# Output projection of a two-layer encoder from seven block products instead of eight, with weight sums made by adding loads

## The chip, the core and the metric

The kernel runs on one core of a Trainium2 chip. The metric is the device time of one launch in microseconds (us), the median over several runs. The core has a matrix engine (PE), a vector engine (DVE), a scalar engine (ACT), a general engine (POOL) and a queue engine (SP) that issues loads and stores; POOL's queue can issue them too. Each engine works its own instructions in the order in which they stand, and waits on semaphores for the others. Operands lie in SBUF, 128 partitions wide; PE writes its sums into PSUM.

## The reference, cut to what matters

```python
D_MODEL = 1024; SEQ = 512; DEPTH = 2
def reference(x, w_in, pre_g, post_g, ..., w_branch, gate_b, w_out):
    for l in range(DEPTH):
        xn = rmsnorm(x, pre_g[l])
        proj = xn @ w_in[l]
        ...
        br = jnp.einsum('bsnc,ncd->bsnd', ys, w_branch[l])
        gates = jax.nn.sigmoid(g_logits.reshape(B, S, N_BRANCH, D) + gate_b[l])
        merged = jnp.sum(gates * br, axis=2)
        x = x + rmsnorm(merged @ w_out[l], post_g[l])
    return x
```

`merged @ w_out[l]` is the output projection: 512 x 1024 by 1024 x 1024, once in each layer, all in float32.

## The kernel before

Every float32 product is made of three matmuls. Each operand is split into a high part, rounded to the type that PE reads, and a low part, the rest; `mm3` multiplies high by high, high by low and low by high. For a weight tile (128 x 1024), `split_raw` does the split: ACT casts the loaded tile into `whi` (line 102), then DVE or POOL subtracts that from the loaded tile into `wlo` (line 107). With `pool=True` the subtractions go to DVE and POOL in turn, with `pool=False` to DVE alone. Four buffers each hold `whi` and `wlo`, three hold loaded tiles, and three PSUM buffers (`pm`) hold the sums of a unit while they are read.

A layer ends with two stages. The gate stage makes the merged rows `mrg`, feature by feature (8 groups of 128 features, `m`, by 512 rows); its last group is finished by DVE at line 254. The output projection follows. Before it, every `mrg[:, m]` is split into `A_h` (ACT, line 700) and `A_l` (DVE, line 701). Then for each half `hf` of the output columns (512) four weight tiles are loaded (512 KB each) and split with `pool=False`, and for each block `tb` of 128 rows a unit of 24 matmuls, 128 x 512, runs. ACT squares the unit's sum with an accumulator (line 725), DVE multiplies it by the post-norm weight (line 727). After the second half, DVE adds the two accumulators (line 135), POOL raises to the power -0.5 (line 136), and DVE writes the block's new rows with two instructions (line 735), which SP stores.

In layer 0 the next layer's first step is woven in: `norm_x(tb)` squares the new rows (ACT, line 160), scales them (DVE, line 164), has PE transpose them (line 167) and splits the result into `A_h` (ACT, line 172) and `A_l` (DVE, line 173). After it comes `mla_down`, the first projection of the next layer, with four weight tiles of 128 x 832 (`wqd`, split at lines 102 and 107) and 24 matmuls of 416 columns for each block. The last unit of layer 1 is cut into two halves of 256 columns.

The order on an engine is not the order of the source alone: a scheduler sets it when the kernel is built, by what it takes each instruction to last. It is the same on every run.

The loop of the projection:

```python
for hf in range(2):
    po = [split_w(wout[l, hf, j], 1024, False) for j in range(4)]
    for tb in range(TB):
        ...
        for k, (c0, c1) in enumerate(parts):
            ps = tm_unit(po, BW, tb, c0, c1)[:, :c1 - c0]
            if hf == 1 and l < L - 1 and tb > 0:
                norm_x(tb - 1, cl[l + 1])
            s_.activation(out=tmp_t()[:, :c1 - c0], in_=ps, func=AF.Square, ...)
            v_.tensor_tensor(out=o[:, c0:c1], in0=ps, in1=pg[hf][:, c0:c1], op=ALU.mult)
```

Of the kernel before, what the change touches and what calls it, by code (L numbers as in the profile page):

```python
# [40 lines left out]
def trunk_kernel(ctx, tc, x, wtm, wqd, wrv, wqk, wfm, wgate, wbr, wout,  # L41
# [555 lines left out]

    for l in range(L):
        c = cl[l]
        qk, zc, zb, st = {}, {}, {}, {}  # L600
# [98 lines left out]
        for m in range(KT):
            s_.activation(out=A_h[:, m, :], in_=mrg[:, m, :], func=AF.Copy, scale=0.25)  # L700
            v_.scalar_tensor_tensor(out=A_l[:, m, :], in0=mrg[:, m, :], scalar=0.25, in1=f32(A_h[:, m, :]),
                                    op0=ALU.mult, op1=ALU.subtract)
# [6 lines left out]
        sss = []  # L709
        for tb in range(TB):  # L710
            nc.sync.dma_start(out=x_rows(tb), in_=xsrc[tb * P:(tb + 1) * P, :].rearrange("p (a b) -> p a b", a=2))
        for hf in range(2):
# [1 line left out]
            for tb in range(TB):

                parts = [(0, 256), (256, 512)] if (l, hf, tb) == (L - 1, 1, TB - 1) else [(0, 512)]
                if hf == 0:
                    sss.append(small("sso", 3))
                ss = sss[tb]
                o = YT[:, tb, :] if hf == 0 else tmp_t()  # L720
                for k, (c0, c1) in enumerate(parts):
                    ps = tm_unit(po, BW, tb, c0, c1)[:, :c1 - c0]
                    if hf == 1 and l < L - 1 and tb > 0:
                        norm_x(tb - 1, cl[l + 1])
                    s_.activation(out=tmp_t()[:, :c1 - c0], in_=ps, func=AF.Square, scale=D ** -0.5,
                                  accum_out=ss[:, hf + k:hf + k + 1])
                    v_.tensor_tensor(out=o[:, c0:c1], in0=ps, in1=pg[hf][:, c0:c1], op=ALU.mult)
                if hf == 0:
                    continue
                if len(parts) == 2:  # L730
                    v_.tensor_tensor(out=ss[:, 1:2], in0=ss[:, 1:2], in1=ss[:, 2:3], op=ALU.add)
                r = rstd_rows(ss)
                xr = x_rows(tb)
                for k, src in enumerate((YT[:, tb, :], o)):
                    v_.scalar_tensor_tensor(out=xr[:, k, :], in0=src, scalar=r[:, 0:1], in1=xr[:, k, :],
                                            op0=ALU.mult, op1=ALU.add)
                    nc.sync.dma_start(out=xdst[tb * P:(tb + 1) * P, k * 512:(k + 1) * 512], in_=xr[:, k, :])
# [85 lines left out]
```

## Time and profile before

| what | value |
|---|---|
| median of 3 runs | 1084.35 us (1083.19 to 1084.37) |
| the profiled execution | 1084.56 us |
| its span, first to last instruction | 1082.8 us |
| PE busy | 1057.6 us, 98% of the span, 5096 matmuls |
| DVE busy | 645.8 us, 60% |
| ACT busy | 529.7 us, 49% |
| POOL busy | 234.2 us, 22% |
| output projection | about 499 to 546 us (layer 0), 1032 to 1077 us (layer 1) |

Busy time is the time in which an engine has an instruction running. A row of the timeline gives start, duration, engine, line, operation and `out<-in`; `xN` joins N instructions in a row; in brackets stands how long the engine sat idle before it and what released it. Matmuls overlap: one lasts longer than the distance to the next, and the distance is what it costs.

### The profile page before, as it was taken

The page shows a single profiled execution, that of the slowest core. Times are in us where ns is not written, and L with a number is a line of the kernel's source. Part 1 is how long each engine was busy: PE and PEld are TensorE (multiplying, and loading weights), DVE is VectorE, ACT ScalarE, POOL GpSimd, SP SyncE. Part 2 cuts the span into 40 slices and gives each one's busy share as a digit, 9 for nine tenths or more (in the row PEclk, how much of TensorE's full clock was granted, in tenths as well). Part 3 has the DMA queues.
Part 4 walks back from the last instruction along what each step waited for, and adds up shares of the span by engine and source line. Part 5 has one row for each costly group of instructions (what it writes and reads, how often), then busy time and mean ns, then how long its engine had stood idle before and what let it go on. Part 6 is the DMA issues. An engine that isn't in the chain of part 4 may idle for free.

```text
span 1082.8 us, 14199 instructions
## 1 busy us (share of the span) xinstructions
PE 1057.6 (98%) x5096; PEld 885.7 (82%) x5096; DVE 645.8 (60%) x1332; ACT 529.7 (49%) x1073; POOL 234.2 (22%) x249
## 2 busy tenths in 40 slices
PE   6999999999999999999999999999999999999997
PEld 5887878888888888888788787788888888888886
DVE  5774776666466654345577756675666665634443
ACT  6444576555454553224573644664544545432331
POOL 2311132221123232210033111331212323221000
PEclk9999999999999999999999999999999999999999
DMA  7221132223232223334343222213223322323342
GB/s 242 79 102 59 55 105 81 70 87 107 78 98 88 78 88 107 98 114 159 106 136 101 99 76 66 88 59 88 88 78 107 88 82 86 105 78 98 107 156 78
DMA packets 37703, 104.65 MB, mean 97 GB/s; under 512 B 5376, under 2 KB 6400, under 8 KB 37632
## 3 DMA queue, kind: packets, MB, share of 16 engines
q1 hardware_dynamic: 37632, 103.74, 30.6%
q8 instruction: 40, 0.66, 0.2%
q14 instruction: 31, 0.25, 0.1%
HBM read 99.53 MB, written 4.19 MB: 96 GB/s over the span
## 4 chain that ended last, share of the span: by engine, by line
PE 43%; ACT 3%; DVE 2%; issue 1%; DMA 1%; POOL 1%; POOLq 0%; DVEq 0%; ACTq 0%
PE pm L114 12%; PE pm L113 12%; PE pm L115 12%; PE pt L361 2%; PE po L379 1%; PE po L378 1%; DMA wraw<-in_wgate_dram 0%; ACT whi L102 0%; PE ps_s L419 0%; PE ps_s L418 0%; PE ps_s L436 0%; PE ps_s L438 0%; PE ps_s L437 0%; ACT tmp L160 0%; DMA wraw<-in_sgu_wt_dram 0%
## 5 line engine op out<-in xcount | busy, mean ns | idle before, releaser
L102 ACT CAST whi<-wraw 128x1024 fp32r<-128x1024 f32 (+3 forms) x194 | 177.4, 916 | 250.8 <-PE pm L114 149.0
L113 PE MATMUL pm<-A_h,whi 128*128 128x512 f32 x640 | 257.0, 402 | 0.0
L115 PE MATMUL pm<-A_h,wlo 128*128 128x512 f32 x640 | 249.8, 390 | 0.0
L114 PE MATMUL pm<-A_l,whi 128*128 128x512 f32 x640 | 249.5, 390 | 0.0
L107 DVE TENSOR_TENSOR wlo<-wraw,whi 128x1024 fp32r<-128x1024 f32 (+3 forms) x130 | 152.1, 1172 | 108.6 <-ACT whi L102 107.5
L107 POOL TENSOR_TENSOR wlo<-wraw,whi 128x1024 fp32r<-128x1024 f32 (+1 forms) x64 | 116.2, 1815 | 370.2 <-ACT whi L102 303.6
L113 PE MATMUL pm<-whi,A_h 128*128 128x512 f32 (+2 forms) x456 | 176.6, 388 | 2.2 <-ACT A_h L172 2.2
L114 PE MATMUL pm<-wlo,A_h 128*128 128x512 f32 (+2 forms) x456 | 175.1, 384 | 1.1 <-DVE wlo L107 1.0
L115 PE MATMUL pm<-whi,A_l 128*128 128x512 f32 (+2 forms) x456 | 175.0, 384 | 0.4
L115 PEld LDWEIGHTS pm<-A_h,wlo 128*128 128x128 f32 x640 | 120.2, 188 | 26.0
L114 PEld LDWEIGHTS pm<-A_l,whi 128*128 128x128 f32 x640 | 120.5, 188 | 22.4
L113 PEld LDWEIGHTS pm<-A_h,whi 128*128 128x128 f32 x640 | 120.3, 188 | 22.0
L113 PEld LDWEIGHTS pm<-whi,A_h 128*128 128x128 f32 x456 | 86.1, 189 | 19.0 <-ACT A_h L172 4.1
L114 PEld LDWEIGHTS pm<-wlo,A_h 128*128 128x128 f32 x456 | 86.4, 189 | 16.6 <-DVE wlo L107 2.6
L115 PEld LDWEIGHTS pm<-whi,A_l 128*128 128x128 f32 x456 | 86.1, 189 | 16.5 <-DVE A_l L173 1.9
L354 DVE TENSOR_SCALAR pp<-pp,st 128x128 f32<-128x128 f32 (+3 forms) x128 | 70.3, 549 | 3.6
L367 ACT CAST PT_h<-pt 128x128 fp32r<-128x128 f32 (+3 forms) x128 | 54.0, 423 | 29.6 <-PE pt L361 28.7
L368 DVE TENSOR_TENSOR PT_l<-pt,PT_h 128x128 fp32r<-128x128 f32 (+3 forms) x128 | 61.6, 481 | 6.7 <-ACT PT_h L367 6.3
L423 DVE CUSTOM_DVE_ANT_0 pp<-ps_s,bk 128x128 f32<-128x128 f32 (+1 forms) x64 | 31.2, 488 | 56.7 <-PE ps_s L419 56.3
L361 PE MATMUL pt<-ident,pp 128*128 128x128 f32 x320 | 55.8, 272 | 1.5 <-DVE X L212 1.5
L444 ACT ACTIVATE pp<-ps_s,st 128x128 f32<-128x128 f32 (+1 forms) x64 | 33.9, 529 | 43.6 <-DVE st L442 43.0
L426 ACT ACTIVATE pp<-pp,st 128x128 f32<-128x128 f32 (+1 forms) x64 | 36.0, 563 | 38.0 <-DVE st L425 37.5
(180 smaller groups left out, 1578.6 us busy)
## 6 DMA issues: line engine op xcount, KB each, us to landing
wraw<-in_wgate_dram SPq DMA_DIRECT2D x48, 512.0 KB, 3.6
wraw<-in_wtm_dram SPq DMA_DIRECT2D x32, 512.0 KB, 3.5
wraw<-in_wfm_dram SPq DMA_DIRECT2D x32, 512.0 KB, 3.6
wraw<-in_wbr_dram SPq DMA_DIRECT2D x48, 256.0 KB, 2.6
wraw<-in_wout_dram SPq DMA_DIRECT2D x16, 512.0 KB, 3.6
bk<-in_rel_dram SPq DMA_DIRECT2D x16, 256.0 KB, 2.7
wraw<-in_wqd_dram SPq DMA_DIRECT2D x8, 416.0 KB, 4.6
mrg<-in_x_dram SPq DMA_DIRECT2D x8, 256.0 KB, 6.1
```

What stands on the lines that cost most here:

```text
L102: s_.copy(out=hi[:, :cols], in_=raw[:, :cols])
L107: i = e.tensor_tensor(out=lo[:, :cols], in0=raw[:, :cols], in1=f32(hi[:, :cols]), op=ALU.subtract)
L113: t_.matmul(out=ps, lhsT=lh, rhs=rh, start=start, stop=False)
L114: t_.matmul(out=ps, lhsT=lh, rhs=rl, start=False, stop=False)
L115: t_.matmul(out=ps, lhsT=ll, rhs=rh, start=False, stop=stop)
L354: v_.tensor_scalar(out=pp[:, :n], in0=pp[:, :n], scalar1=rc, scalar2=None, op0=ALU.mult)
L361: t_.transpose(pt[:, kb * P:(kb + 1) * P], pp[:, kb * P:(kb + 1) * P], ident)
L367: s_.copy(out=dst(PT_h), in_=src)
L368: v_.tensor_tensor(out=dst(PT_l), in0=src, in1=f32(dst(PT_h)), op=ALU.subtract)
L423: v_.tensor_tensor_reduce(out=pp[:, :n], in0=ps[:, :n], in1=bias[:, S - n:S], scale=1.0, scalar=-3e38, op0=ALU.add, op1=ALU.max, accum_out=mx)
L426: s_.activation(out=pp[:, :n], in_=pp[:, :n], func=AF.Exp, bias=nm, accum_out=se)
L444: s_.activation(out=pp[:, :n], in_=ps[:, :n], func=AF.Exp, bias=nm, accum_out=se)
```

## The change

The four quarters of the merged rows (256 rows x 512 features: A11, A12, A21, A22) and of the weights (512 x 512) are combined as in Strassen's form in Winograd's variant. Seven products, Q1 to Q7, of a quarter by a quarter replace eight; each is two units (`b`) of 12 matmuls, 128 x 512. Q1, Q2 and Q4 take a plain quarter on the row side, Q5, Q6, Q7 and Q3 differences of quarters (`U1` to `U4`): eight subtractions on DVE over SBUF (line 744 of the new kernel), and 14 splits of 512 columns where there were eight (ACT 717, DVE 718). On the weight side SP loads two quarters into the buffer `vt`, which the attention no longer needs (slots `sa` and `sb`, line 702). They serve Q1 and Q3; then POOL's queue adds further quarters to them in place (`added`, line 771), which gives the weights of Q5, Q6 and Q4 in `sa` and of Q7 in `sb`: eight loads of 512 KB in each layer. Each waits until the tile's former content has been split, and the next split waits for it. Q2 takes its quarter through `wraw`. All of these tiles are split with `pool=True`.

On the output side ACT copies the sums of Q1 and Q5 out of PSUM (lines 813 and 823), DVE adds or subtracts the others from them (`total`, line 806), and the square and the multiplication (lines 786 and 788) read SBUF. Rows of blocks 0 and 1 are complete after Q6, those of blocks 2 and 3 after Q4, the last product. In layer 0 `norm_x` of blocks 0 and 1 is called inside Q7, of blocks 2 and 3 after the first and second step of `mla_down`.

```diff
+    def vt_tile(dt):
+        return cst.tile([P, TB, 2 * BW], dt, name="vt", tag="vt")
...
+        room = vt_tile(F32)
+        sa, sb = [[room[:, 2 * i + j, :] for j in range(2)] for i in range(2)]
+        for slot, k0, hf in ((sa, 0, 0), (sb, 4, 1)):
+            for j in range(2):
+                nc.sync.dma_start(out=slot[j], in_=wout[l, hf, k0 // 2 + j])
...
+        def split_q(hi, lo, src):
+            s_.activation(out=hi, in_=src, func=AF.Copy, scale=0.25)
+            v_.scalar_tensor_tensor(out=lo, in0=src, scalar=0.25, in1=f32(hi), op0=ALU.mult, op1=ALU.subtract)
...
+        def difference(dst, a, b):
+            fs = pairs([f_tile("uf"), f_tile("uf")])
+            for k in range(2):
+                v_.tensor_tensor(out=fs[k], in0=a(k), in1=b(k), op=ALU.subtract)
+                split_q(dst[0][k], dst[1][k], fs[k])
+            return fs, operands(*dst)
...
+        A11 = quarter(0, QA)
+        A12 = quarter(4, QA)
+        f1, U1 = difference(yb_tiles(), mq(0, QB), mq(4, QB))
+        f2, U2 = difference(yb_tiles(), mq(0, QA), lambda k: f1[k])
+        f4, U4 = difference(x_tiles(0), mq(4, QA), lambda k: f2[k])
+        f3, U3 = difference(x_tiles(4), mq(0, QB), mq(0, QA))
+        A22 = quarter(4, QB)
...
-            po = [split_w(wout[l, hf, j], 1024, False) for j in range(4)]
...
+        def added(slot, k0, hf):
+
+            for j in range(2):
+                g_.dma_start(out=slot[j], in_=wout[l, hf, k0 // 2 + j], accum_op=ALU.add)
+
+        def split_s(slot):
+            return [split_raw(t, 1024, True) for t in slot]
...
+        def row_part(tb, hf, src, o, c0=0, c1=BW):
+
+            s_.activation(out=tmp_t()[:, :c1 - c0], in_=src, func=AF.Square, scale=D ** -0.5,
+                          accum_out=sss[tb][:, hf + 2 * (c0 > 0):hf + 2 * (c0 > 0) + 1])
+            v_.tensor_tensor(out=o[:, c0:c1], in0=src, in1=pg[hf][:, c0:c1], op=ALU.mult)
+            return o
+
+        def rows_out(tb, os):
+            r = rstd_rows(sss[tb])
...
+                v_.scalar_tensor_tensor(out=xr[:, k, :], in0=src, scalar=r[:, 0:1], in1=xr[:, k, :],
+                                        op0=ALU.mult, op1=ALU.add)
...
+        def unit(U, w, b, c0=0, c1=BW):
+            ps = main()[:, :c1 - c0]
+            product(ps, U, w, b, c0, c1)
+            return ps
+
+        def total(a, b, op=ALU.add, out=None):
+            f = f_tile("sum") if out is None else out
+            v_.tensor_tensor(out=f, in0=a, in1=b, op=op)
+            return f
...
+        w1 = split_s(sa)
+        w2 = [split_w(wout[l, 0, 2 + j], 1024) for j in range(2)]
+        q1, q5 = [f_tile("q1"), f_tile("q1")], []
+        for b in range(2):
+            s_.copy(out=q1[b], in_=unit(A11, w1, b))
+        added(sa, 0, 1)
+        w5 = split_s(sa)
+        o1 = []
+        for b in range(2):
+            o1.append(row_part(b, 0, total(unit(A12, w2, b), q1[b]), o=YT[:, b, :]))
+        added(sa, 4, 1)
+        w3 = split_s(sb)
+        for b in range(2):
+            q5.append(f_tile("q5"))
+            s_.copy(out=q5[b], in_=unit(U1, w5, b))
+        added(sb, 0, 1)
+        w6 = split_s(sa)
+        q53 = [total(unit(U4, w3, b), q5[b]) for b in range(2)]
+        added(sa, 4, 0)
+        w7 = split_s(sb)
+        for b in range(2):
+            total(unit(U2, w6, b), q1[b], ALU.subtract, q1[b])
+            o = row_part(b, 1, total(q53[b], q1[b], ALU.add, q53[b]), o=tmp_t())
+            rows_out(b, ((0, o1[b]), (1, o)))
+        w4 = split_s(sa)
+        o2 = []
+        for b in range(2):
+            ps = unit(U3, w7, b)
+            if l < L - 1:
+                norm_x(b, cl[l + 1])
+            total(ps, q1[b], ALU.add, q1[b])
+            o2.append(row_part(2 + b, 1, total(q1[b], q5[b], ALU.add, q5[b]), o=YT[:, 2 + b, :]))
...
+                f = total(unit(A22, w4, b, c0, c1), q1[b][:, c0:c1], ALU.subtract, q1[b][:, c0:c1])
+                row_part(tb, 0, f, o, c0, c1)
...
             dgen = mla_down(l + 1, st1, [])
+            step(dgen)
+            norm_x(TB - 2, cl[l + 1])
             step(dgen)
             norm_x(TB - 1, cl[l + 1])
```

Lines of the new kernel are named by its own numbers; up to line 600 they are those of before plus two (`whi` 104, `wlo` 109, the gate's last sum 256, the norm's square 162, its scaling 166, its `A_l` 175, the accumulators' sum 137).

**First place: the start of the projection in layer 0.** On ACT before, the last merged group is split (row 385) and the first three units are squared out of PSUM at once:

```order
383 L239 ACTIVATE tmp<-pm,gbh_106 128x512
384 L102 CAST whi<-wraw 128x1024
385 L700 ACTIVATE A_h<-mrg 128x512
386 L725 ACTIVATE tmp,sso<-pm 128x512 x3
387 L102 CAST whi<-wraw 128x1024 x3
```

On ACT now (`uf` are the differences, `ybh` and `X` their high parts, `q_4652` and `q_4653` the copies of Q1's two units):

```order
386 L717 ACTIVATE A_h<-mrg 128x2x256 x2
387 L717 ACTIVATE ybh<-uf 128x512 x2
388 L104 CAST whi<-vt 128x1024
389 L717 ACTIVATE ybh<-uf 128x512
390 L104 CAST whi<-vt 128x1024
391 L717 ACTIVATE X<-uf 128x512 x3
392 L813 COPY q_4652<-pm 128x512
393 L813 COPY q_4653<-pm 128x512
```

The two copies that empty Q1's PSUM buffers stand behind three splits of differences (row 391). On DVE now, from the gate's last sum (row 601) on:

```order
601 L256 TENSOR_TENSOR mrg<-mrg,tmp 128x512
602 L744 TENSOR_TENSOR uf<-mrg 128x512
603 L744 TENSOR_TENSOR uf<-mrg,uf 128x512
604 L718 SCALAR_TENSOR_TENSOR A_l<-mrg,A_h 128x2x256
605 L718 SCALAR_TENSOR_TENSOR ybl<-uf,ybh 128x512 x2
606 L744 TENSOR_TENSOR uf<-mrg,uf 128x512 x3
607 L718 SCALAR_TENSOR_TENSOR ybl<-uf,ybh 128x512
608 L744 TENSOR_TENSOR uf<-mrg 128x512
609 L718 SCALAR_TENSOR_TENSOR X<-uf,X 128x512 x3
```

The third split of ACT's row 391 reads what DVE's row 608 writes, ten instructions after row 601.

**Second place: POOL's queue over the projection of layer 0.** Before, POOL has no weight tile there, only the powers of line 136 (row 113):

```order
112 L107 TENSOR_TENSOR wlo<-wraw,whi 128x512 x6
113 L136 TENSOR_TENSOR rs<-rs,mhalf 128x1 x6
114 L283 AFFINE_SELECT wraw<-wraw 128x1024
115 L136 TENSOR_TENSOR rs<-rs,mhalf 128x1
116 L128 TENSOR_SCALAR rs<-ss 128x1
```

Now (the DMA rows are the adding loads; rows 114 to 125 belong to Q1, Q2, Q5, Q3, Q6, Q7 and Q4 in this order):

```order
113 L771 DMA vt<-in_wout_dram 128x1024
114 L109 TENSOR_TENSOR wlo<-vt,whi 128x1024
115 L771 DMA vt<-in_wout_dram 128x1024
116 L109 TENSOR_TENSOR wlo<-wraw,whi 128x1024
117 L109 TENSOR_TENSOR wlo<-vt,whi 128x1024
118 L771 DMA vt<-in_wout_dram 128x1024 x2
119 L109 TENSOR_TENSOR wlo<-vt,whi 128x1024
120 L771 DMA vt<-in_wout_dram 128x1024 x3
121 L109 TENSOR_TENSOR wlo<-vt,whi 128x1024
123 L109 TENSOR_TENSOR wlo<-vt,whi 128x1024
124 L138 TENSOR_TENSOR rs<-rs,mhalf 128x1
125 L109 TENSOR_TENSOR wlo<-vt,whi 128x1024
```

Seven subtractions over a weight tile and eight loads have come to this engine in each layer.

**Third place: DVE at the seam between the layers.** Before, the low parts of the next layer's first weights (128x832) stand among the splits of the norm, three of them ahead of the last block's sum (row 643, `rs<-sso`):

```order
633 L173 SCALAR_TENSOR_TENSOR A_l<-pt,col_324,A_h 128x128 x2
634 L107 TENSOR_TENSOR wlo<-wraw,whi 128x832
637 L107 TENSOR_TENSOR wlo<-wraw,whi 128x832
639 L107 TENSOR_TENSOR wlo<-wraw,whi 128x832
641 L727 TENSOR_TENSOR tmp<-pm,bk 128x512
643 L135 SCALAR_TENSOR_TENSOR rs<-sso 128x1
644 L107 TENSOR_TENSOR wlo<-wraw,whi 128x832
```

Now (row 650 reads the last unit of Q4 out of PSUM, rows 654 and 661 are the sums of blocks 2 and 3):

```order
650 L806 TENSOR_TENSOR q_4653<-pm,q_4653 128x512
652 L788 TENSOR_TENSOR tmp<-q_4652,bk 128x512
654 L137 SCALAR_TENSOR_TENSOR rs<-sso 128x1
655 L788 TENSOR_TENSOR tmp<-q_4653,bk 128x512
656 L175 SCALAR_TENSOR_TENSOR A_l<-pt,col_324,A_h 128x128 x2
657 L795 SCALAR_TENSOR_TENSOR mrg<-YT,rs,mrg 128x512
659 L795 SCALAR_TENSOR_TENSOR mrg<-tmp,rs,mrg 128x512
661 L137 SCALAR_TENSOR_TENSOR rs<-sso 128x1
662 L109 TENSOR_TENSOR wlo<-wraw,whi 128x832
663 L795 SCALAR_TENSOR_TENSOR mrg<-YT,rs,mrg 128x512
665 L109 TENSOR_TENSOR wlo<-wraw,whi 128x832 x3
```

The first low part of `wqd` (row 662) has moved behind the last unit's reading and its block's sum.

## Rows read from the trace of the kernel before

**Rows 1.** The page, part 1: busy us, share of the span, instructions.
```profile
PE 1057.6 (98%) x5096; PEld 885.7 (82%) x5096; DVE 645.8 (60%) x1332; ACT 529.7 (49%) x1073; POOL 234.2 (22%) x249
```
**Rows 2.** Busy time in the projection of layer 0: PE, PEld, DVE, ACT, POOL, clock, DMA.
```profile
499.60:546.00 46.40, 45.50 (x206) 36.81 (x205) 24.19 (x47) 20.67 (x50) 2.75 (x5) 1.00 0.35 122
```
**Rows 3.** Timeline of DVE, two units of the projection.
```profile
505.30 0.69 DVE L727 TENSOR_TENSOR YT<-pm,bk 128x512 f32<-128x512 f32 x1 [2.94 <-ACT tmp L725]
510.74 0.69 DVE L727 TENSOR_TENSOR YT<-pm,bk 128x512 f32<-128x512 f32 x1 [4.75 <-ACT tmp L725]
```
**Rows 4.** Timeline of PE, half units of 256 columns.
```profile
1070.67 0.28 PE L113 MATMUL pm<-whi,A_h 128*128 128x256 f32 x1
...
1071.15 0.28 PE L114 MATMUL pm<-wlo,A_h 128*128 128x256 f32 x1
```
**Rows 5.** Timeline of DVE, the end of the gate stage in layer 0.
```profile
494.15 3.69 DVE L701 SCALAR_TENSOR_TENSOR A_l<-mrg,A_h 128x512 fp32r<-128x512 f32 x6
...
499.93 0.69 DVE L254 TENSOR_TENSOR mrg<-mrg,tmp 128x512 f32<-128x512 f32 x1
```
**Rows 6.** Timeline of ACT at the end of the projection's first unit.
```profile
504.58 0.60 ACT L725 ACTIVATE tmp<-pm 128x512 f32<-128x512 f32 x1 [3.29 <-PE pm L115]
```
**Rows 7.** Timeline of DVE, three instructions that started while POOL ran one.
```profile
339.49 1.36 DVE L354 TENSOR_SCALAR pp<-pp,st 128x128 f32<-128x128 f32 x1
...
398.29 0.69 DVE L252 SCALAR_TENSOR_TENSOR tmp<-tmp,pm 128x512 f32<-128x512 f32 x1 [3.02 <-PE pm L115]
...
483.61 1.56 DVE L254 TENSOR_TENSOR mrg<-mrg,tmp 128x512 f32<-128x512 f32 x1
```
**Rows 8.** Timeline of POOL at the same three times.
```profile
338.36 2.40 POOL L107 TENSOR_TENSOR wlo<-wraw,whi 128x1024 fp32r<-128x1024 f32 x1 [3.51 <-ACT whi L102]
...
396.46 2.40 POOL L107 TENSOR_TENSOR wlo<-wraw,whi 128x1024 fp32r<-128x1024 f32 x1 [4.29 <-ACT whi L102]
...
483.33 1.29 POOL L107 TENSOR_TENSOR wlo<-wraw,whi 128x512 fp32r<-128x512 f32 x1 [6.87 <-ACT whi L102]
```
**Rows 9.** Timeline of DVE at the seam between the layers.
```profile
542.40 0.75 DVE L735 SCALAR_TENSOR_TENSOR mrg<-YT,rs,mrg 128x512 f32<-128x512 f32 x1 [0.41 <-POOL rs L136]
...
547.68 0.88 DVE L164 TENSOR_SCALAR tmp<-mrg,rs 128x512 f32<-128x512 f32 x2 [0.44 <-POOL rs L136]
...
550.36 0.61 DVE L173 SCALAR_TENSOR_TENSOR A_l<-pt,col,A_h 128x128 fp32r<-128x128 f32 x2
...
550.96 1.02 DVE L107 TENSOR_TENSOR wlo<-wraw,whi 128x832 fp32r<-128x832 f32 x1
```
**Rows 10.** Waits of PE from 495 to 580 us: total us, times, longest.
```profile
PE pt L167 <- DVE tmp L164: 3.1, 4, 1.8
```
**Rows 11.** Timeline of PE and DVE at the end of the kernel.
```profile
1076.31 0.28 PE L115 MATMUL pm<-whi,A_l 128*128 128x256 f32 x1
...
1077.18 0.42 DVE L727 TENSOR_TENSOR tmp<-pm,bk 128x256 f32<-128x256 f32 x1 [2.42 <-ACT tmp L725]
```
**Rows 12.** The page, part 6: KB each, us from issue to landing.
```profile
wraw<-in_wout_dram SPq DMA_DIRECT2D x16, 512.0 KB, 3.6
...
mrg<-in_x_dram SPq DMA_DIRECT2D x8, 256.0 KB, 6.1
```
**Rows 13.** Busy time after the last matmul, columns as in rows 2.
```profile
1079.00:1080.00 1.00, 0.00 (x0) 0.00 (x0) 0.94 (x2) 0.00 (x0) 0.00 (x0) 1.00 0.00 0
1080.00:1081.00 1.00, 0.00 (x0) 0.00 (x0) 0.00 (x0) 0.00 (x0) 0.00 (x0) 0.79 0.87 322
```
**Rows 14.** Timeline of PE, its first matmuls of the kernel and later ones alike.
```profile
10.93 0.71 PE L113 MATMUL pm<-whi,A_h 128*128 128x416 f32 x1 [2.06 <-ACT A_h L172]
...
14.98 0.55 PE L114 MATMUL pm<-wlo,A_h 128*128 128x416 f32 x1
...
16.87 0.36 PE L114 MATMUL pm<-wlo,A_h 128*128 128x416 f32 x1
17.07 0.35 PE L115 MATMUL pm<-whi,A_l 128*128 128x416 f32 x1
```

More of the change, by code (lines that the diff above doesn't have):

```diff
@@ L67, in trunk_kernel @@
     cos, sin = csn[:, :, 0:HALF], csn[:, :, HALF:ROPE]
-    vt = cst.tile([P, TB, 2 * BW], F32R, name="vt")
+    def vt_tile(dt):
+        return cst.tile([P, TB, 2 * BW], dt, name="vt", tag="vt")
     PT_h = cst.tile([P, TB * PTS + P], F32R, name="PT_h")
@@ L599, in trunk_kernel @@
         c = cl[l]
+        vt = vt_tile(F32R)
         qk, zc, zb, st = {}, {}, {}, {}
@@ L696, in trunk_kernel, with quarter, pairs, f_tile @@
         run(gc)
[L699 to L702, printed above, removed]
+        QA, QB = slice(0, 256), slice(256, 512)
+        def split_q(hi, lo, src):
+            s_.activation(out=hi, in_=src, func=AF.Copy, scale=0.25)
+            v_.scalar_tensor_tensor(out=lo, in0=src, scalar=0.25, in1=f32(hi), op0=ALU.mult, op1=ALU.subtract)
+        def quarter(k0, t):
+            for k in (k0, k0 + 2):
+                split_q(A_h[:, k:k + 2, t], A_l[:, k:k + 2, t], mrg[:, k:k + 2, t])
+            return [(A_h[:, k, t], A_l[:, k, t]) for k in range(k0, k0 + 4)]
+        def pairs(tiles):
+            return [t.rearrange("p (k t) -> p k t", k=2) for t in tiles]
+        def f_tile(nm):
+            return wk.tile([P, S], F32, name=nm, tag="qk", bufs=12)
+        def operands(hs, ls):
+            return [(h[:, k, :], w[:, k, :]) for h, w in zip(hs, ls) for k in range(2)]
+        def yb_tiles():
+            y = [yb_pair() for _ in range(2)]
+            return pairs([t[0] for t in y]), pairs([t[1] for t in y])
+        def x_tiles(k0):
+            return pairs([X[:, k0, :], X[:, k0 + 1, :]]), pairs([X[:, k0 + 2, :], X[:, k0 + 3, :]])
+        def difference(dst, a, b):
[4 more added lines that the diff above has]
+            return fs, operands(*dst)
+        def mq(k0, t):
+            return lambda k: mrg[:, k0 + 2 * k:k0 + 2 * k + 2, t]
+        A11 = quarter(0, QA)
[5 more added lines that the diff above has]
+        A22 = quarter(4, QB)
         pg = []
@@ L708, in trunk_kernel @@
         xsrc, xdst = (x, x1) if l == 0 else (x1, out)
-        sss = []
         for tb in range(TB):
             nc.sync.dma_start(out=x_rows(tb), in_=xsrc[tb * P:(tb + 1) * P, :].rearrange("p (a b) -> p a b", a=2))
-        for hf in range(2):
-            po = [split_w(wout[l, hf, j], 1024, False) for j in range(4)]
[L714 to L737, printed above, removed]
@@ new lines, in trunk_kernel, with product @@
+        sss = [small("sso", 4) for _ in range(TB)]
+        def added(slot, k0, hf):
[3 more added lines that the diff above has]
+            return [split_raw(t, 1024, True) for t in slot]
+        def product(ps, U, w, b, c0=0, c1=BW):
+            tbs = slice(b * P, (b + 1) * P)
+            for j, (hi, lo) in enumerate(w):
+                for kk in range(2):
+                    k = 2 * j + kk
+                    cs = slice(kk * BW + c0, kk * BW + c1)
+                    mm3(ps, U[k][0][:, tbs], U[k][1][:, tbs], hi[:, cs], lo[:, cs], k == 0, k == 3)
@@ new lines, in row_part @@
+        def row_part(tb, hf, src, o, c0=0, c1=BW):
[5 more added lines that the diff above has]
+            r = rstd_rows(sss[tb])
+            xr = x_rows(tb)
+            for k, src in os:
+                v_.scalar_tensor_tensor(out=xr[:, k, :], in0=src, scalar=r[:, 0:1], in1=xr[:, k, :],
+                                        op0=ALU.mult, op1=ALU.add)
+                nc.sync.dma_start(out=xdst[tb * P:(tb + 1) * P, k * 512:(k + 1) * 512], in_=xr[:, k, :])
@@ new lines, in trunk_kernel @@
+        for b in range(2):
+            tb = 2 + b
+            parts = [(0, 256), (256, 512)] if (l, b) == (L - 1, 1) else [(0, 512)]
+            o = tmp_t()
+            for c0, c1 in parts:
+                f = total(unit(A22, w4, b, c0, c1), q1[b][:, c0:c1], ALU.subtract, q1[b][:, c0:c1])
+                row_part(tb, 0, f, o, c0, c1)
+            if len(parts) == 2:
+                v_.tensor_tensor(out=sss[tb][:, 0:1], in0=sss[tb][:, 0:1], in1=sss[tb][:, 2:3], op=ALU.add)
+            rows_out(tb, ((1, o2[b]), (0, o)))
```

## The prediction, as it was put on record before the run

> **What bounds the kernel now.** I read the page first: PE is busy 1057.6 us of 1082.8, 98%, and no other engine passes 60% [rows 1]. So the time is the number of matmuls times their distance, plus whatever PE waits. The busy time of the projection's own stretch says the same from nearby: PE 45.50 of 46.40 us at granted clock 1.00, DVE 24.19, ACT 20.67, POOL 2.75 [rows 2]. Two things follow. Matmuls taken out there shorten the kernel one for one, as long as nothing new makes PE wait; and DVE, half idle on average, may still be late in places, since what counts is where its work stands. The list of PE's waits shows how little is late today: 3.1 us around the seam between the layers, for the norm's scaling [rows 10].
>
> Durations are those of the profiled execution, 1084.56 us, which is 0.2 us above the median of the runs; the sum is made against it.
>
> **Matmuls removed.** In layer 0, 8 units of 24 become 14 of 12: 24 fewer of 512 columns. In layer 1, where the last unit is halved, 12 fewer of 512 and 24 fewer of 256. Two units lie 5.44 us apart [rows 3], so one matmul costs 5.44 / 24 = 0.227 us; four of 256 columns take 0.48 us [rows 4], 0.12 each. 36 x 0.227 + 24 x 0.12 = **-11.0 us**. This is all that the change can win.
>
> **Start of the projection: the third PSUM buffer.** PE runs Q1's two units and Q2's first into the three `pm` buffers, 3 x 12 x 0.227 = 8.2 us after its first matmul, which I call t0. Q2's second unit needs the buffer of Q1's first, and that is free when ACT has copied it (ACT's row 392). The copy stands behind three splits of differences, the third of which needs DVE's row 608, ten instructions after the gate's last sum. Before, the first unit's square starts at 504.58 [rows 6]; a unit's 5.44 and the 0.16 by which a matmul outlasts its distance [rows 4] earlier is 499.0, so t0 is 499.0 on this clock, and the gate's last sum ends at 499.93 + 0.69 [rows 5], t0 + 1.6. DVE instructions over 512 columns follow one another at 3.69 / 6 = 0.615 us [rows 5]: ten take 6.2, so t0 + 7.8, then a split and a copy on ACT at 0.6 each, as its square of the same width [rows 6]: t0 + 9.0, with some hand-offs 9.4. That alone is a stall of 1.2 us in each layer.
>
> It grows by POOL. Two of its new weight tiles fall into this chain (POOL's rows 116 and 117), 2.40 us each [rows 8]. What DVE does beside such an instruction, the timelines show: a sum that started 0.28 us into a POOL instruction of 1.29 took 1.56 us instead of 0.69; a small one started inside POOL's 2.40 and ended 0.09 after it; one whose second input is in PSUM took its usual 0.69 beside another of 2.40 [rows 5, 7, 8]. The ten instructions read SBUF only. So each POOL tile can hold the chain for up to 2.4 us; bounds for the stall are 1.2 and 6.0 us in each layer. The first tile may have begun before the chain, the second gets in between two of its instructions and costs nearly all; I take 5.0, **+10 us** for both layers. The Trainium skill ("SBUF — State Buffer", section "Who interferes with whom") says of such a pair that whichever was issued first keeps the shared port and the other is fully blocked. If DVE's unbroken chain always came first by that rule, POOL would wait in its place, which is the second rival below.
>
> **Adding loads.** No row shows one. The nearest are the 512 KB loads of the same weights, 3.6 us, and the slowest class on the page, 6.1 [rows 12]. The tightest turn is Q6's: its two loads may start when Q5's tiles are split and must be there, split again, some 8 us later, three units on. Up to about 6 us they cost nothing, and I take that; the cover is those three units. The Trainium skill ("DMA: Bandwidth & Descriptors", section "Anatomy of one DMA — SWDGE (gpsimd) path") gives 2.0 us plus bytes by 436 GB/s for plain loads of that queue, an estimate of 3.2 us here, and no price for adding; by it this term is zero too. SP's four loads into `vt` stand in its queue ahead of the gate's weights, long before Q1 wants them: nothing.
>
> **The seam between the layers.** The first low part of the next layer's weights (DVE's row 662) now stands behind the last unit of Q4 and its block's sum; before, three of the four stood ahead of that. Call E the end of Q4's last matmul. DVE can begin with Q4's first total (row 640) 2.7 us earlier, and rows 640 to 662 hold six instructions at 0.615 (3.7), 16 splits of the norm at 0.61 / 2 (4.9), two scalings at 0.44 (0.9), two row writings at 0.7 (1.4), three sums of one column (0.3) and the low part, 1.02 [rows 5, 9]: 12.2 us, so it ends at about E + 9.6. PE has one matmul and eight transposes to do meanwhile, about 1.2, and waits some 8.4. The waits of the transposes that were there (3.1 [rows 10]) come back for blocks 2 and 3, and the next low parts (row 665), behind the block's writing, add some 0.6. Below, if DVE had nothing queued: total 0.7, square 0.8, sum 0.2, low part 1.0 after E, a wait of 1.7 that replaces 3.1. Bounds -1.4 and +10; the row count is the nearer: **+9 us**.
>
> **The end of layer 1.** From the end of Q6's first unit PE has 2.7 + 5.4 + 5.4 = 13.6 us left. DVE has nine totals and five multiplications at 0.615 (8.6), two halves of each at 0.4 (1.6), eight row writings at 0.7 (5.6) and two low parts of 1024 columns at 1.02 x 1024 / 832 (2.5): 18.3. So it ends some 4.7 us later relative to PE than before, and the last half's total adds 0.4 ahead of the square [rows 9, 11]. Bounds: 0.4 if it starts ahead, 7.5 if a POOL tile holds it too. **+5 us**.
>
> **The clock.** After the last matmul (1076.59 [rows 11]) the granted clock read 1.00 in the third microsecond and 0.79 in that which begins 3.4 us after it [rows 13]. The kernel's first matmuls came at (14.98 - 10.93) / 10 = 0.405 us, later ones alike at 0.20 [rows 14]: ten cost 2 us more. So a stall as long as the seam's can cost 2 us beyond itself; **+2 us** for that one. The two stalls of 5 us are near it, and left to a rival.
>
> Sum: -11.0 + 10 + 9 + 5 + 2 = +15; 1084.56 + 15 = **1100 us**.
>
> **Rivals.**
> - *DVE is in time (faster).* Everything hangs on whether DVE reaches row 662 by E + 1.2 and row 608 by t0 + 7. For it: DVE is half idle over the stage [rows 2]. Then the stalls are 2 x 1.2, the seam -1.4, the end 0.4: -11.0 + 2.4 - 1.4 + 0.4 = -9.6, 1075 us. It decides at the seam: with less than about 8 us of wait there and no held chain the kernel is faster. Against: 12.2 us of instructions in a row, counted.
> - *No held chain.* POOL waits for DVE instead of DVE for POOL: -11.0 + 2.4 + 9 + 5 + 2 = +7.4, 1092 us. Against: DVE waited in every such pair that I looked at [rows 7, 8].
> - *The clock falls in all three stalls, which are of full length.* -11.0 + 12 + 10 + 5 + 6 = +22, 1107 us. For it: 6.0 is longer than the 3.4 to 4.4 after which the clock was lower [rows 13]. The Trainium skill ("TensorE: Matmul & The Clock Gate", section "HAM oscillation — how this bites in real kernels") says that waits of PE throttle it again, and that the next stretch begins cold. That speaks for this case, and the trace agrees as far as the kernel's end goes, 0.79 there.
> - *Adding loads are slow.* If they land after 12 us, Q6 and Q4 wait 4 to 6 us each in each layer: another 16 to 24, 1116 to 1124 us. No row speaks for or against it.
>
> **How the numbers follow.** My case 0.42; clock and full stalls 0.18; no held chain 0.14; slow adding loads 0.12; DVE in time 0.10; something between that ends within 0.2% (2 us, about what a measurement can tell) 0.04. The range reaches from 1087, below the case of no held chain, to 1114; outside lie the faster case, the even one and half of the slow loads, 0.20. Faster 0.10, same 0.04, slower 0.86.
>
> **What would show it.** PE's waits in the new profile: one of about 5 us for an ACT copy at Q2's second unit in each layer; one of 8 us at the seam for a low part of 128x832 on DVE; DVE subtractions of 128x512 that last 2 to 3 us beside POOL's tiles of 2.40; PE's busy time down by about 11; the stretch from the last matmul to the end longer than 6.2 us. I am wrong if the adding loads appear among PE's waits by way of the casts, if the copies are in time, or if PE's first wait at the seam is under 3 us.

## The result and the profile after

The changed kernel takes 1111.7 us, median of 4 runs (1109.85 to 1113.38), against 1083.86 us before on the same chips: a ratio of 1.0257, 95% interval 1.0237 to 1.0277. It is 28 us slower; 1100 was forecast, with a range up to 1114. The profiled execution is the fastest of the four (1109.85 us); its span grew from 1082.8 to 1108.1, by 25.3 us, and that is what the account below explains.

Page of the changed kernel, part 1, as in [rows 1], and the granted clock in 40 slices of part 2:

```profile
span 1108.1 us, 14202 instructions
...
PE 1057.3 (95%) x5036; PEld 881.4 (80%) x5036; DVE 697.3 (63%) x1387; ACT 551.0 (50%) x1105; POOL 296.9 (27%) x279
...
PEclk9999999999999999999989999999999999999997
```

PE has 60 matmuls less and yet the same busy time as in [rows 1]: something made the others longer. The clock has an 8 in the slice that holds the end of the seam (554 to 582 us). The waits of PE in the changed kernel (line waited for: us in total, times, longest):

```profile
PE pt L169 <- DVE tmp L166: 13.0, 4, 6.7
PE pm L116 <- DVE wlo L109: 9.0, 6, 5.4
PE pm L115 <- ACT q L813: 5.8, 2, 2.9
PE pm L115 <- DVE q L806: 3.6, 2, 2.6
PE pm L116 <- POOL wlo L109: 3.3, 2, 1.7
```

The 6.7 of the first row is the kernel's start and was there before (6.9). The rest are the forecast's places and one more. Where each ends, in PE's timeline:

```profile
509.80 0.68 PE L115 MATMUL pm<-whi,A_h 128*128 128x512 f32 x1 [2.88 <-ACT q L813]
510.28 0.63 PE L116 MATMUL pm<-wlo,A_h 128*128 128x512 f32 x1
510.71 0.63 PE L117 MATMUL pm<-whi,A_l 128*128 128x512 f32 x1
...
513.55 0.40 PE L115 MATMUL pm<-whi,A_h 128*128 128x512 f32 x1
513.78 0.40 PE L116 MATMUL pm<-wlo,A_h 128*128 128x512 f32 x1
...
521.17 0.50 PE L116 MATMUL pm<-wlo,X 128*128 128x512 f32 x1 [1.07 <-DVE wlo L109]
...
529.86 0.50 PE L116 MATMUL pm<-wlo,ybh 128*128 128x512 f32 x1 [1.59 <-POOL wlo L109]
...
546.82 1.31 PE L169 MATMUL pt<-ident,tmp 128*128 128x128 f32 x8 [4.08 <-DVE tmp L166]
...
559.31 0.72 PE L116 MATMUL pm<-wlo,A_h 128*128 128x416 f32 x1 [5.36 <-DVE wlo L109]
...
1096.44 0.39 PE L115 MATMUL pm<-whi,A_h 128*128 128x256 f32 x1 [2.64 <-DVE q L806]
...
1098.48 0.42 PE L117 MATMUL pm<-whi,A_l 128*128 128x256 f32 x1
```

From top to bottom: Q2's second unit waits 2.88 us for a copy, and the matmuls behind it come 0.43 us apart until 513.3, then 0.23 again; the granted clock reads 0.51 from 511.0 to 513.4 us, the lower of its two levels (1.2 instead of 2.4 GHz). Q3 waits 1.07, Q6 1.59, both for low parts. At the seam the transposes of block 0 wait 4.08 and the next layer's first low part 5.36. Layer 1 repeats the first three (2.88, 1.05, 1.72). The last matmul starts 9.6 us before the span's end; before, 6.5 [rows 11].

The account, in us of the span (measured: waits of the timeline, less those of before at the same places; the matmuls removed are counted, at the distances that the prediction took):

| term | forecast | measured | how |
|---|---|---|---|
| matmuls removed | -11.0 | -11.0 | 36 and 24 fewer, counted |
| Q2's second unit | +10 | +5.8 | 2 x 2.88 |
| Q3 and Q6 | 0 | +5.4 | 1.07 + 1.59 + 1.05 + 1.72 |
| seam | +9 | +9.3 | 4.08 + 0.42 + 5.36 + 0.34 + 1.97 + 0.29, less 3.1 [rows 10] |
| end of layer 1 | +5 | +6.7 | 0.93 + 2.64, and 9.6 - 6.5 |
| slow clock | +2 | +8 | some 45 matmuls 0.1 to 0.2 us farther apart |

With 0.16 us of hand-off at each of a dozen waits this makes 26; the span says 25.3.

### The profile page after: what moved, and what is told of

Read it like the earlier page. It is cut to its first block, busy times and chain, and to the rows that moved or that the text cites. A ratio compares the mean times of both kernels' runs of the same rounds, so it can differ in the third digit from the quotient of the medians.

```text
span 1108.1 us, 14202 instructions
## 1 busy us (share of the span) xinstructions
PE 1057.3 (95%) x5036; PEld 881.4 (80%) x5036; DVE 697.3 (63%) x1387; ACT 551.0 (50%) x1105; POOL 296.9 (27%) x279
## 4 chain that ended last, share of the span: by engine, by line
PE 79%; DVE 6%; ACT 5%; POOL 4%; DMA 3%; issue 2%; SPq 0%; POOLq 0%; DVEq 0%; ACTq 0%
PE pm L115 22%; PE pm L116 22%; PE pm L117 22%; PE pt L363 3%; POOL wlo L109 2%; PE po L381 2%; PE po L380 2%; DMA vt<-in_wout_dram 1%; DVE mrg L795 1%; ACT whi L104 1%; PE ps_s L438 1%; PE ps_s L440 1%; PE ps_s L439 1%; PE ps_s L421 1%; PE ps_s L420 1%
## 5 line engine op out<-in xcount | busy, mean ns | idle before, releaser
L104 ACT CAST whi<-wraw 128x1024 fp32r<-128x1024 f32 (+3 forms) x182 | 164.9, 907 | 234.9 <-PE pm L116 139.1
L109 POOL TENSOR_TENSOR wlo<-wraw,whi 128x512 fp32r<-128x512 f32 (+1 forms) x66 | 122.2, 1852 | 376.2 <-ACT whi L104 302.9
L109 DVE TENSOR_TENSOR wlo<-wraw,whi 128x1024 fp32r<-128x1024 f32 (+3 forms) x116 | 135.0, 1166 | 97.1 <-ACT whi L104 96.5
L115 PE MATMUL pm<-whi,A_h 128*128 128x512 f32 (+2 forms) x372 | 148.5, 399 | 11.6 <-ACT q L813 5.8
L116 PE MATMUL pm<-wlo,A_h 128*128 128x512 f32 (+2 forms) x372 | 146.6, 394 | 6.9 <-DVE wlo L109 6.9
L117 PE MATMUL pm<-whi,A_l 128*128 128x512 f32 (+2 forms) x372 | 146.4, 394 | 0.4
L115 PEld LDWEIGHTS pm<-whi,A_h 128*128 128x128 f32 x372 | 72.2, 194 | 28.4 <-ACT q L813 6.6
L116 PEld LDWEIGHTS pm<-wlo,A_h 128*128 128x128 f32 x372 | 72.5, 195 | 19.6 <-DVE wlo L109 8.2
L117 PEld LDWEIGHTS pm<-whi,A_l 128*128 128x128 f32 x372 | 72.7, 195 | 14.7 <-DVE A_l L175 2.5
```

What stands on the lines that cost most here:

```text
L104: s_.copy(out=hi[:, :cols], in_=raw[:, :cols])
L109: i = e.tensor_tensor(out=lo[:, :cols], in0=raw[:, :cols], in1=f32(hi[:, :cols]), op=ALU.subtract)
L115: t_.matmul(out=ps, lhsT=lh, rhs=rh, start=start, stop=False)
L116: t_.matmul(out=ps, lhsT=lh, rhs=rl, start=False, stop=False)
L117: t_.matmul(out=ps, lhsT=ll, rhs=rh, start=False, stop=stop)
```

## The experiments

Each was timed beside the kernel before on the same chip, whose median was 1083.8 to 1084.5 us; four of them (five PSUM buffers, plain loads with all low parts on DVE, spare matmuls at the seam, the seam's order) ran on another chip than the kernel that they build on. Runs of one kernel spread by 1 to 4 us, so differences of 1 to 2 us between two experiments are read from the traces, not from the times.

**POOL's tiles: all low parts on DVE.** In the changed kernel DVE and POOL both stretch. Timeline of DVE, then of POOL, in the projection of layer 0:

```profile
499.59 0.69 DVE L256 TENSOR_TENSOR mrg<-mrg,tmp 128x512 f32<-128x512 f32 x1
500.31 2.79 DVE L744 TENSOR_TENSOR uf<-mrg 128x512 f32<-128x512 f32 x1
503.02 0.68 DVE L744 TENSOR_TENSOR uf<-mrg,uf 128x512 f32<-128x512 f32 x1
...
507.84 0.68 DVE L744 TENSOR_TENSOR uf<-mrg 128x512 f32<-128x512 f32 x1
508.44 1.88 DVE L718 SCALAR_TENSOR_TENSOR X<-uf,X 128x512 fp32r<-128x512 f32 x3
510.25 0.68 DVE L744 TENSOR_TENSOR uf<-mrg 128x512 f32<-128x512 f32 x1
510.85 0.68 DVE L718 SCALAR_TENSOR_TENSOR A_l<-mrg,A_h 128x512 fp32r<-128x512 f32 x1
511.45 1.21 DVE L109 TENSOR_TENSOR wlo<-vt,whi 128x1024 fp32r<-128x1024 f32 x1
512.59 0.68 DVE L718 SCALAR_TENSOR_TENSOR X<-uf,X 128x512 fp32r<-128x512 f32 x1
513.19 0.68 DVE L806 TENSOR_TENSOR sum<-pm,q 128x512 f32<-128x512 f32 x1
...
516.61 4.50 DVE L109 TENSOR_TENSOR wlo<-vt,whi 128x1024 fp32r<-128x1024 f32 x1
...
537.20 2.88 DVE L795 SCALAR_TENSOR_TENSOR mrg<-YT,rs,mrg 128x512 f32<-128x512 f32 x1 [0.46 <-POOL rs L138]
```

```profile
499.76 2.79 POOL L109 TENSOR_TENSOR wlo<-wraw,whi 128x1024 fp32r<-128x1024 f32 x1 [4.18 <-ACT whi L104]
507.79 7.75 POOL L109 TENSOR_TENSOR wlo<-vt,whi 128x1024 fp32r<-128x1024 f32 x1 [5.24 <-ACT whi L104]
515.84 1.76 POOL L771 DMA_DIRECT2D vt<-in_wout_dram  x2 [0.30 <-POOL wlo L109]
516.98 3.04 POOL L109 TENSOR_TENSOR wlo<-vt,whi 128x1024 fp32r<-128x1024 f32 x1
```

POOL's first tile began before DVE's first difference and held it for 2.1 us. The second came into an unbroken chain of DVE and was itself held, 7.75 us instead of 2.40, and Q6's adding loads, next in POOL's queue, left only at 515.84. It ended 2.35 us after DVE's first total over PSUM (513.19) had begun, about its own length, as if it had got its turn only there; up to then all of DVE's inputs lay in SBUF. The same distance is 2.34 us in layer 1. The Trainium skill ("SBUF — State Buffer", section "Who interferes with whom") says that the order of issue decides who blocks. The first tile agrees. The second does so only in part: eight of DVE's instructions that began after it still went ahead of it. DVE's subtraction of 4.50 us, where 1.2 is usual, doesn't fit: it began 0.37 us before POOL's third tile and yet ended 1.1 us after it, and this stays unexplained.

```diff
-            return [split_raw(t, 1024, True) for t in slot]
+            return [split_raw(t, 1024, False) for t in slot]
...
-        w2 = [split_w(wout[l, 0, 2 + j], 1024) for j in range(2)]
+        w2 = [split_w(wout[l, 0, 2 + j], 1024, False) for j in range(2)]
```

> Edit: the low parts of all the projection's weight tiles are made on DVE, none on POOL. Theory 1 (POOL's tiles and DVE's instructions over SBUF hold each other up): DVE's first difference takes 0.7 instead of 2.8 us, the first row writing 0.75 instead of 2.88, and no unit waits for a low part from POOL; the waits at Q2 shrink to about 1 us and with them the slow stretches: 8 to 13 us faster than the changed kernel, 1099 to 1104 us. Rival (DVE has no time left): seven more tiles of 1.2 us on DVE in each layer make it the later one, 1112 to 1120 us.

Measured: 1098.97 us, 12.7 less, ratio to before 1.014 (1.0125 to 1.0155). DVE does more and the kernel is faster. In its timeline of DVE the first difference and the first row writing are back at their usual lengths:

```profile
503.55 0.68 DVE L744 TENSOR_TENSOR uf<-mrg 128x512 f32<-128x512 f32 x1
...
534.65 0.75 DVE L795 SCALAR_TENSOR_TENSOR mrg<-YT,rs,mrg 128x512 f32<-128x512 f32 x1 [0.47 <-POOL rs L138]
```

Q2's wait falls to 1.71 us (the prediction had 1.2 for it without POOL's tiles), those of Q3 and Q6 are gone, block 0's transposes wait 1.97 instead of 4.08; the seam's low part stays at 5.43. Theory 1 holds. The experiments from here on that start at 1099.0 build on this kernel.

**ACT's order: Q1's copies first.** On the changed kernel:

```diff
-        f4, U4 = difference(x_tiles(0), mq(4, QA), lambda k: f2[k])
-        f3, U3 = difference(x_tiles(4), mq(0, QB), mq(0, QA))
-        A22 = quarter(4, QB)
...
             s_.copy(out=q1[b], in_=unit(A11, w1, b))
+        f4, U4 = difference(x_tiles(0), mq(4, QA), lambda k: f2[k])
+        f3, U3 = difference(x_tiles(4), mq(0, QB), mq(0, QA))
+        A22 = quarter(4, QB)
```

> Edit: the differences for Q3 and Q7, the split of A22 and the loads over the merged rows are written behind Q1's two copies, so that ACT copies Q1's sums out of PSUM before it splits those differences. Theory 1 (the copies' place in ACT's order makes the wait of 2.88 us at Q2's second unit): both waits for the copies go (5.8 us) and so does the slow stretch behind each (about 1.6 us each): some 9 us faster than the changed kernel, about 1103 us. Rival (DVE's chain of differences and splits is what is late, and ACT's order only shows it): the wait moves on to Q5 or Q3, which then wait for their low parts on DVE by about as much: 1109 to 1113 us.

Measured: 1107.07 us, 4.6 less; between the two. The waits for the copies are gone, but Q5 now waits 3.71 us in each layer for the same POOL tile, with a slow stretch behind it again (granted clock 0.50 from 515.0 to 518.5 us), and only the small waits of Q3 and Q6 vanish with it. From its list of PE's waits:

```profile
PE pm L116 <- POOL wlo L109: 7.4, 2, 3.7
```

So about half of what theory 1 gave to the place of the copies came back as a wait for POOL's tile.

**A deeper PSUM.** Five buffers in turn instead of three:

```diff
-            ps = main()[:, :c1 - c0]
+            turn[0] += 1
+            ps = main() if turn[0] % 5 < 3 else pss.tile([P, S], F32, name="ps_s", tag="ps_s")
+            ps = ps[:, :c1 - c0]
...
+        turn = [-1]
```

> Edit, on top of the kernel with all low parts on DVE (1099.0 us): the units take turns over five PSUM buffers instead of three (the attention's two are free in this stage). Theory 1 (the third buffer is what Q2's second unit waits for): the 1.7 us waits for the copies go in both layers and the end of layer 1 loses its 1.0 us wait for DVE: 1094.5 to 1096 us. Rival (PE then only waits a product later, for operands from DVE's chain): 1098 to 1099.5 us.

Measured: 1099.68 us, no gain. Q2 waits no more; Q5 waits 1.01 for a cast and 0.64 for a low part, in each layer. The rival holds: PE runs ahead to the next operand that ACT and DVE have not made.

**The adding loads.** On the changed kernel, and on the one with all low parts on DVE:

```diff
-                g_.dma_start(out=slot[j], in_=wout[l, hf, k0 // 2 + j], accum_op=ALU.add)
+                nc.sync.dma_start(out=slot[j], in_=wout[l, hf, k0 // 2 + j])
```

> Edit: the eight adding loads of each layer become plain loads of the same bytes on SP's queue; the addition is left out, so the weights of Q5, Q6, Q7 and Q4 are single quarters and the output is not that of the reference. It prices the adding. Theory 1 (adding loads, 5.7 us to landing and up to 1 us of POOL each, make Q6 late): the wait of 1.6 to 1.7 us for Q6's low part goes in both layers, and POOL's tiles begin earlier: 3 to 6 us faster than the changed kernel, 1106 to 1109 us. Rival (the loads are hidden, what is late is the tile on POOL ahead of them): within 1 us, 1111 to 1113 us.

> Edit, on top of the kernel with all low parts on DVE (1099.0 us): the adding loads become plain loads on SP's queue, the addition left out, so that the weights of Q5, Q6, Q7 and Q4 are single quarters. Theory 1 (the adding loads are hidden once POOL makes no tiles; in the changed kernel they were late because POOL, which issues them, was held): 1098 to 1099.5 us. Rival (their landing of 5.7 us against 3.6 is itself on the path): 3 us or more faster, below 1096.5 us.

Measured: 1104.34 us (7.4 less, more than theory 1 of that run allowed; the waits at Q3 and Q6 are gone in both layers) and 1093.87 us (5.1 less, the rival of that run). So the adding loads are on the path even where POOL makes no tiles. On the page of the changed kernel, part 6, they take 5.7 us to landing (the median; 5.5 to 8.8):

```profile
vt<-in_wout_dram POOLq DMA_DIRECT2D x16, 512.0 KB, 5.7
```

The 3.6 of plain loads [rows 12] is not the figure to set beside this, since loads land later in this stage. With all low parts on DVE, the six loads issued between 500 and 545 us take 7.5 us (median) when they add, 4.8 when they are plain. In that kernel ACT sits idle for them before its casts, as in these two rows of its timeline:

```profile
520.07 1.05 ACT L104 CAST whi<-vt 128x1024 fp32r<-128x1024 f32 x1 [2.70 <-DMA vt<-in_wout_dram]
...
531.18 1.05 ACT L104 CAST whi<-vt 128x1024 fp32r<-128x1024 f32 x1 [2.18 <-DMA vt<-in_wout_dram]
```

The sums of one slot are a chain: split, load onto it, split again. These gaps don't show as PE waiting for a DMA; they make the casts late, the low parts behind them, and DVE's work bunches. What of this is the adding and what the queue is left open: the edit changes both at once.

**The clock.** Spare matmuls in the wait of Q2's second unit (changed kernel), and in the wait at the seam (all low parts on DVE):

```diff
+            if b == 1:
+                spare = tpsum()
+                for _ in range(4):
+                    for kk in range(3):
+                        t_.matmul(out=spare, lhsT=A11[0][0][:, 0:P], rhs=w2[0][0][:, 0:BW],
+                                  start=kk == 0, stop=kk == 2)
             o1.append(row_part(b, 0, total(unit(A12, w2, b), q1[b]), o=YT[:, b, :]))
```

```diff
+            spare = pss.tile([P, S], F32, name="ps_s", tag="ps_s")
+            for i in range(20):
+                t_.matmul(out=spare, lhsT=A_h[:, 1, P:2 * P], rhs=X[:, 0, :], start=i == 0, stop=i == 19)
             step(dgen)
             norm_x(TB - 2, cl[l + 1])
```

> Edit: twelve spare matmuls of 512 columns into a PSUM buffer that nothing reads, right ahead of Q2's second unit in each layer, where PE waits 2.88 us. They take 12 x 0.227 = 2.7 us. Theory 1 (PE's idling lowers its clock for the stretch behind the wait, in which eight matmuls came at 0.43 instead of 0.23 us): with PE kept busy the stretch runs at full clock, 1.6 us less in each layer, 1108 to 1109 us. Rival (the slow stretch has another cause, such as PSUM or operands that come late): the eight matmuls stay slow, 1112 us.

> Edit, on top of the kernel with all low parts on DVE (1099.0 us): twenty spare matmuls of 512 columns into a PSUM buffer that nothing reads, placed in the 5.4 us wait at the seam; they use operands that are there and hold up no buffer that is wanted. Theory 1 (PE's idling lowers its clock): the 13 matmuls of 416 columns behind the wait, at 0.35 us each, come at 0.19: about 2 us less, 1096.5 to 1097.5 us. Rival (the slow pace behind a wait is not the clock, or the wait ends as late because something else is late): 1098.5 to 1100 us.

Measured: 1110.7 us (1.0 less, within the runs' spread) and 1097.78 us (1.2 less); both lie between the theory's time and the rival's. The clock did what theory 1 says, the time did not follow it. Busy time from 510 to 515 us, PE, PEld, DVE, ACT, POOL, clock, DMA, first in the changed kernel, then with the spare matmuls:

```profile
510.00:515.00 5.00, 5.00 (x16) 3.95 (x16) 4.42 (x7) 2.41 (x4) 5.00 (x1) 0.66 0.83 267
```

```profile
510.00:515.00 5.00, 4.65 (x19) 3.49 (x19) 4.97 (x8) 3.00 (x7) 5.00 (x1) 1.00 0.85 265
```

0.66 became 1.00, and the matmuls behind come at 0.23. But Q5, reached sooner, now waits 1.1 us for POOL's long tile. At the seam the matmuls behind the spare ones come at 0.19 instead of 0.35 us, PE's timeline there:

```profile
549.39 5.71 PE L857 MATMUL ps_s<-X,A_h 128*128 128x512 f32 x20 [0.37 <-ACT A_h L174]
554.94 0.35 PE L116 MATMUL pm<-wlo,A_h 128*128 128x416 f32 x1
555.12 0.35 PE L117 MATMUL pm<-whi,A_l 128*128 128x416 f32 x1
555.31 0.34 PE L115 MATMUL pm<-whi,A_h 128*128 128x416 f32 x1
```

and part of the 2 us comes back as a longer wait of the next transposes (2.57 instead of 1.98). The two traces also differ ahead of the spare matmuls: behind the 1.97 us that block 0's transposes wait, the granted clock reads 0.61 without them and 1.00 with them, so the 1.2 us is not theirs alone. Keeping PE busy kept the clock up, then; but it pays only where PE is what is late.

**The seam.** The next layer's first two tiles split ahead of the last rows:

```diff
+        ready = [split_w(wqd[l + 1, j], 832, False) for j in range(2)] if l < L - 1 else []
         for b in range(2):
             tb = 2 + b
...
-            dgen = mla_down(l + 1, st1, [])
+            dgen = mla_down(l + 1, st1, [], ready=ready)
```

> Edit, on top of the kernel with all low parts on DVE (1099.0 us): the first two weight tiles of the next layer are split ahead of the last two row blocks' sums, so that DVE makes their low parts before it finishes those rows. Theory 1 (the place of these low parts in DVE's order makes the 5.4 us wait at the seam): the wait shrinks by 2 us or more and the norm of the later blocks is not much delayed: 1094 to 1097 us. Rival (DVE has a fixed amount of work at the seam, and what goes ahead of one thing delays another): the wait moves to the transposes of blocks 2 and 3, 1098 to 1100 us.

Measured: 1097.1 us, 1.9 less; between the two, next to theory 1. The profiled execution took 1100.27 us, 3 us above the median, so its waits can't be set against that gain. In it the wait of 5.4 us becomes 3.33, as theory 1 says, and the transposes of block 2 wait 3.18 instead of 1.98, followed by another slow stretch, as the rival says: 1.2 of the 2.1 us that the one wait loses come back in the other.

**DVE's amount of work.** Multiplications left out:

```diff
-            v_.tensor_tensor(out=o[:, c0:c1], in0=src, in1=pg[hf][:, c0:c1], op=ALU.mult)
-            return o
+            return src
...
+            o = q1[b]
```

> Edit, on top of the kernel with all low parts on DVE (1099.0 us): DVE's eight multiplications by the post-norm weight in each layer are left out, so that part of the result is missing; nothing else moves but what the scheduler makes of it. They take 0.6 us each, 4.8 us in each layer. Theory 1 (DVE, not PE, sets the end of both projections): the time falls by most of what stands late, 5 to 9 us, 1090 to 1094 us. Rival (PE's waits come from single places in the order, DVE has room otherwise): at most 2 us, 1097 us or more.

Measured: 1089.84 us, 9.1 less, about the 2 x 4.8 us that they take on DVE, and at the upper end of theory 1. Not all of it is DVE's own time: the seam has one slow stretch in place of two, worth some 2 us. The seam's 5.4 us wait for a low part is down to 0.6; of its list of PE's waits:

```profile
PE pm L116 <- DVE wlo L109: 3.5, 6, 1.1
```

So most of what is taken from DVE in these stages comes off the kernel. DVE's share of busy time, 63%, doesn't show this; these stages do. Summing Q2 onto Q1 in PSUM, which would take totals off DVE, was not tried.

**Layer 1 alone.** Layer 0's projection as before (the loop over `hf`), layer 1's with seven products:

```diff
+        if l == 0:
+            for hf in range(2):
+                po = [split_w(wout[l, hf, j], 1024, False) for j in range(4)]
...
+        else:
+            A11 = quarter(0, QA)
```

> Edit: layer 0 as in the kernel before, layer 1 with seven products and all low parts on DVE. Layer 1 has no seam behind it. Theory 1 (from the traces: in that kernel layer 1's matmuls end 0.5 us sooner after the gate's last sum than before, and the end after them is 4.2 us longer): 3 to 5 us slower than before, 1087 to 1089 us, so even without the seam the form doesn't pay. Rival (layer 1 loses only because it enters behind a disturbed layer 0): 1083 to 1085 us.

Measured: 1088.39 us, ratio 1.0038 (1.0023 to 1.0053). In its timelines of DVE and PE the gate's last sum and the last matmul are

```profile
1033.07 0.69 DVE L256 TENSOR_TENSOR mrg<-mrg,tmp 128x512 f32<-128x512 f32 x1
...
1075.37 0.28 PE L117 MATMUL pm<-whi,A_l 128*128 128x256 f32 x1
```

and the sum is in the timeline of before, whose last matmul started at 1076.31 [rows 11],

```profile
1033.23 0.69 DVE L254 TENSOR_TENSOR mrg<-mrg,tmp 128x512 f32<-128x512 f32 x1
```

From the one to the other it takes 42.30 us, before 43.08; from there to the end of the span (1086.0 us) 10.63, before 6.49. Of the 5.6 us of matmuls taken out there, 0.8 are left before the last matmul, the rest went into four waits of PE (1.7 for the copies, 1.0, 0.9, 0.4), and DVE's rest at the end costs 4.1 more. Theory 1 holds; no version that was run is faster than the kernel before.

## Why the prediction was right, point by point

- **What bounds the kernel.** Right: the 60 matmuls are gone, and the waits that came instead decided. Its sign for this, PE's busy time down by about 11, did not show (1057.3 us, before 1057.6), because slow stretches made other matmuls longer.
- **Start of the projection.** The place and the mechanism were right (third PSUM buffer, a copy behind splits behind DVE's chain); the size was not: 5.0 us was taken per layer, 2.88 measured. The step that failed is that POOL's second tile "gets in between two of its instructions and costs nearly all". It did not get in; it waited 5.3 us itself. That was the rival of no held chain, true for one tile of two. What is left of the estimate, 1.2 us and the 2.1 by which the first tile held the chain, is near what was measured.
- **Adding loads.** Wrong: "Up to about 6 us they cost nothing, and I take that". Their median of 5.7 us lies inside that bound, but of Q6's own two one took 7.4 us in layer 0 and 7.6 in layer 1, and the cover had been reckoned from Q5's split on time, while POOL, which splits and issues, was held by DVE. The prediction's own sign of being wrong, adding loads that reach PE's waits by way of the casts, came true. 1.6 and 1.7 us appear at Q6, 1.1 at Q3, and the runs with plain loads put the whole price at 5 to 7 us. The Trainium skill's fit for a DMA that POOL issues ("DMA: Bandwidth & Descriptors", section "Anatomy of one DMA — SWDGE (gpsimd) path"), an estimate of 3.2 us here, is well below the 5.7 measured for adding ones; no run has a plain load on that queue.
- **Seam.** Right in place and cause: DVE's instructions from Q4's first total to the end of the low part were counted as 12.2 us and took about 11.7 (547.6 to 559.3). That the size came out too, 9 forecast and 9.3 measured, is partly luck. For the low part alone 8.4 was forecast and 5.36 measured. What fills the gap was not forecast: block 0's transposes wait 4.08, behind a row writing that took 2.88 us beside POOL's last tile, so that DVE began Q4's first total some 4.2 us ahead of the end of Q4's last matmul (551.8) instead of 2.7.
- **End of layer 1.** Right: 5 forecast, 6.7 measured, inside its bounds (0.4 and 7.5). It is not DVE's surplus alone: here too a row writing took 2.88 us beside a POOL tile, the case that the upper bound stood for.
- **The clock.** Mis-sized: one fall of 2 us was counted, and the rest left to a rival. Four stretches were slow, at 1.6 to 2 us each with a smaller one at the end, 8 us in all. The likeliest case should have had the clock of the rival in which it falls in every stall (+6), though the stalls were shorter than that rival wants.

Against the forecast of +15 the span shows +25: 6 more from the clock, 5.4 from Q3 and Q6 and 1.7 from the end, while the start gave 4 back; the rest is hand-offs. The direction was reasoned and came true. That 1111.7 us lies inside a range up to 1114 owes something to luck: it is 12 us above the likeliest case, the range's upper part was there for full stalls and late loads, and the start's error hid part of the others.

## What to carry to other kernels

Taking a matmul out pays only if the engine that feeds and drains PE has time for what replaces it: here leaving out 16 DVE instructions of 0.6 us took 9.1 us off the whole, some 2 of them by the clock. Count each engine's work against the stage's new, shorter length, stage by stage, before counting what PE saves. And price a long wait of PE with the slow stretch that may follow it: here 1.6 to 2 us behind four of the five waits of 2.6 us and more in the two projections, and 0.7 behind the fifth, where the kernel ended.
